# Both parts of the tokens in one 512-column matmul, for z, 13 query blocks and 20 blocks of u

## The chip, the core and the metric

The kernel runs on one core of one Trainium2 chip. The metric is the device time of the core in microseconds: the median of three runs, 2088.07 us before the change (2087.21 to 2090.55). The engines are named as in the profile: PE is the tensor engine's matmuls and PEld its weight loads, ACT the scalar engine, DVE the vector engine, POOL GpSimd, SP the engine that issues most loads.

## The reference

One decoder layer over 256 tokens and 16 meta tokens, width 2048. What the change touches is cut to this:

```python
proj = h @ w_in                       # [pool 1024 | z 3072 | x 3072 | B 1024 | C 1024 | dt 48]
y = y * silu(z)                       # then a gated RMS norm by group, and w_out
h = layer_norm(ALPHA * h + concat(pool_out, ssd_out) @ w_out)
q = h @ wq                            # 8 heads x 2 x 128, product keys, top 16 experts of 16384
act = gelu(h . u_tab[expert])         # here: h @ u.T for all 16384 experts, masked by the gate
out = layer_norm(ALPHA * h + (gate * act) @ v_tab[expert])
```

All of it is fp32.

## The kernel before, in words

PE multiplies fp32 numbers in three passes. Each operand is split into two parts that PE takes at full speed (fp32r): a high part, rounded by ACT, and a low part, the rest, subtracted by DVE. A product is high x high + token low x weight high + token high x weight low.

The weights of w_in, w_out, wq, u and v stream in 512 KB units, in the order of one list, `W_ORDER`. `next_unit()` hands out the next unit's parts `wh` and `wl` (128 x 1024 each) and keeps three units ahead: SP loads `raw`, ACT casts it to `wh` (line 129), DVE subtracts to `wl` (line 130). There are three buffers of each, so a cast waits until PE has passed the `wh` of the unit three earlier.

For the projections, the queries and u the weight tile is PE's stationary operand and the tokens move. The normed tokens stand transposed as 16 chunks of 128 x 272 (`hTH`, `hTL`, from line 196) or 128 x 256 (`h1H`, `h1L`, line 556). `mm_unit` (line 199) takes one unit, half of the contraction (`kh`), in three passes of eight matmuls, all into the left half of one PSUM bank:

```python
for w, xx, first, last in ((wh, xh, ...), (wh, xl, ...), (wl, xh, ...)):
    for k in range(8):
        pe.matmul(ps[:m, :n], w[:, k * m:(k + 1) * m], xx[:, kh * 8 + k, t0:], ...)
```

A block of 128 output rows is two units. The stages, in order:

- w_in: 72 blocks. Eight groups of five x, B and C blocks and three z blocks (line 477, 256 columns each), with the scan's small steps between them as side work (`tick()`). ACT takes silu of z's bank.
- w_out: here the tokens are stationary and 512 columns of `w` move (`wide_pass`, line 497).
- queries: 16 blocks (line 875). The first three are begun while the tokens are still being normed. ACT copies each bank into `qT` (line 885). DVE then finds the top 16 as side work.
- u: 128 blocks (`u_block`, line 612), 64 for each half of the experts. ACT takes gelu of the bank (line 617 or 620); for the second half DVE multiplies the result into the gate's tile `a` (line 622). For the first half the gate comes later. POOL scatters the blocks of `a` to sorted places in memory (line 719), for the second half one block at a time, as they are done; for the first half from line 728, after DVE has numbered the places (line 711).
- v: the sorted rows are loaded by SP (`ac`, line 990), POOL gathers the rows of v that they name (line 995), and PE multiplies with 512 moving columns (line 1032). The parts of a block of `a` are made by ACT and DVE in `v_scr` (lines 1019 and 1020), which takes the place of `h1L`; the residual `rr` takes the place of `h1H` and is loaded by POOL (line 1105). The tiles of the sorted rows take the place of the second half of `a`.

The order of the instructions on each engine comes from a scheduler at build time, except where the code pins it (`keep_in_program_order`).

Of the kernel before, what the change touches and what calls it, by code (L numbers as in the profile page):

```python
# [11 lines left out]
F32 = mybir.dt.float32  # L12
F32R = mybir.dt.float32r
F16 = mybir.dt.float16
U32 = mybir.dt.uint32
AF = mybir.ActivationFunctionType
# [5 lines left out]
P = 128  # L22
NMETA = 16
NL1 = 3
NQ1 = 3
NLB = 4
NDB = 2

HALF = {1: (64, P - NDB, 52, 12, 39), 0: (0, 64, 53, 13, 40)}
TRIPS = 24
# [12 lines left out]
T = 256  # L45
L = NMETA + T
D = 2048
KC = D // P
# [14 lines left out]
def tile_layer(ctx: ExitStack, tc: tile.TileContext, x, meta, pk, pk48, w_in, w_dt, w_pool,  # L63
               w_out, wq, keys, u, v, ln_nat, out):
    nc = tc.nc
    act, dve, pool, pe = nc.scalar, nc.vector, nc.gpsimd, nc.tensor
# [6 lines left out]
    def ps_tile(name):  # L73
        return psp.tile([P, 512], F32, tag="ps", name=name)
# [13 lines left out]
    def slots_of(half):  # L88
        _, _, n, s, e = HALF[half]
        _, _, top, _ = rows_of(half)  # L90
        return ([(half, k, (0, 1)) for k in range(e - s)], [(half, k, (0,)) for k in range(top - s, top)],
                [(half, k, (1,)) for k in range(e - s, n - s)])

    def mixed(*lists):
        at = [((k + 0.5) / len(one), w, one[k]) for w, one in enumerate(lists) for k in range(len(one))]
        return [b for _, _, b in sorted(at, key=lambda z: z[:2])]

    both, a_only, b_only = zip(slots_of(1), slots_of(0))
    V_BLOCKS = [("d", b, (0, 1)) for b in range(P - NDB, P)] + mixed(both[0], a_only[0], b_only[0][:8])
    LOOP_AT = len(V_BLOCKS)  # L100
    V_BLOCKS += mixed(both[1][:-6], a_only[1], b_only[0][8:] + b_only[1][:-NLB])

    LATE = []
    for k, blk in enumerate(both[1][-6:]):
        V_BLOCKS.append(blk)
        if k < NLB:
            LATE.append(len(V_BLOCKS))
            V_BLOCKS.append(b_only[1][k - NLB])
    for i, (what, b, _) in enumerate(V_BLOCKS):
# [6 lines left out]
    def next_unit():  # L116
        while len(issued) < min(used[0] + 1 + AHEAD, len(W_ORDER)):
            src = W_ORDER[len(issued)]
            wp, wb = held.get(len(issued), (wst, 3))
            if isinstance(src, tuple):  # L120
                n = 1024
                raw = gathered(src[0])[:, src[1] * 1024:(src[1] + 1) * 1024]
            else:
                n = src.shape[-1]
                raw = wst.tile([P, 1024], F32, tag="raw", name="raw", bufs=3)
                nc.sync.dma_start(raw[:, :n], src)
            wh = wp.tile([P, 1024], F32R, tag="wh", name="wh", bufs=wb)
            wl = wp.tile([P, 1024], F32R, tag="wl", name="wl", bufs=wb)
            act.copy(wh[:, :n], raw[:, :n])  # L129
            dve.tensor_sub(wl[:, :n], raw[:, :n], wh[:, :n].bitcast(F32))  # L130
            issued.append((wh, wl))
        used[0] += 1
        r = issued[used[0] - 1]
        issued[used[0] - 1] = None
        return r


    side = []

    def tick(n=1):  # L140
        while n and side:
            try:
                next(side[0])
                n -= 1
            except StopIteration:
                side.pop(0)
# [46 lines left out]

    front = ExitStack()
    hTp = front.enter_context(tc.tile_pool(name="hTp", bufs=1))
    hTH = hTp.tile([P, KC, L], F32R, name="hTH")
    hTL = hTp.tile([P, KC, L], F32R, name="hTL")

    def mm_unit(ps, xh, xl, kh, m, n, t0=0):

        wh, wl = next_unit()
        for w, xx, first, last in ((wh, xh, kh == 0, False), (wh, xl, False, False), (wl, xh, False, kh == 1)):
            for k in range(8):
                pe.matmul(ps[:m, :n], w[:, k * m:(k + 1) * m], xx[:, kh * 8 + k, t0:],  # L204
                          start=first and k == 0, stop=last and k == 7)
# [4 lines left out]
    with tc.tile_pool(name="ln0", bufs=1) as lp:  # L210
# [33 lines left out]
        for k in range(KC):  # L244
            ps = ps_tile("pst")
# [5 lines left out]
            if k == KC // 2 - 1:  # L251

                for t0, m in ((0, NH), (14, P), (14, P)):
                    ps = ps_tile("psj")
# [14 lines left out]
    def proj(t0, m=P):  # L269
        if pre:  # L270
            was, ps = pre.pop(0)
            assert was == t0
            tick()
        else:
            ps = ps_tile("psj")
            mm_unit(ps, hTH, hTL, 0, m, L - t0, t0)
            tick()
        mm_unit(ps, hTH, hTL, 1, m, L - t0, t0)
        tick()
        return ps  # L280
# [183 lines left out]
    _, ps = pre.pop(0)  # L464
# [6 lines left out]
    for g in range(NG):  # L471
        bT = conv(24 + g, 0, "bT", 2)
        cc = conv(32 + g, 12, "cc", 2)
        xT = [conv(3 * g + j, 0, "xT", 6) for j in range(3)]
        zs = []
        side.append(group_steps(g, bT, cc, xT, zs))
        for j in range(3):
            pz = proj(NMETA)
            z = sp.tile([P, T], F32, tag="zs", name="zs", bufs=4)
            act.activation(z, pz[:, :T], AF.Silu)  # L480
            zs.append(z)


# [2 lines left out]
    def hold(units, hp):  # L486
        for i in units:
            held[i] = (hp, len(units))
# [60 lines left out]

    lws = ExitStack()  # L550
    h1ps = []

    def w_out_body1(i):
        if i == 0:
            h1ps.append(ctx.enter_context(tc.tile_pool(name="h1p", bufs=1, side="right", reuse_waits="tile")))
            h1ps.append(h1ps[0].tile([P, KC, T], F32R, tag="h1H", name="h1H"))
            h1ps.append(h1ps[0].tile([P, KC, T], F32R, tag="h1L", name="h1L"))
            lw = lws.enter_context(tc.tile_pool(name="lw", bufs=1, side="right", reuse_waits="tile"))
            hold(range(2 + 144 + 64 - NL1, 2 + 144 + 64), lw)

# [10 lines left out]
                dve.bn_stats(sts[tt][:, c], hs[tt][:, cs])  # L571
    lp = lnp[0]
    lws.close()
    h1p, h1H, h1L = h1ps
    mv = lp.tile([P, 2, 2], F32, name="mv1")
    rs = lp.tile([P, 2], F32, name="rs1")
    nb1 = lp.tile([P, 2], F32, name="nb1")
# [12 lines left out]
    for k in range(KC):  # L590
        ps = ps_tile("pst1")
# [20 lines left out]
    def u_block(b):  # L612
        ps = ps_tile("psu")
        for kh in range(2):
            mm_unit(ps, h1H, h1L, kh, P, T)
        if b < 64:
            act.activation(a_half[0][:, b, :T], ps[:, :T], AF.Gelu)
        else:

            act.activation(ps[:, :T], ps[:, :T], AF.Gelu)  # L620
            g = a_half[1][:, b - 64, :T]
            dve.tensor_mul(g if b < P - NDB else a_dense[:, b - (P - NDB)], g, ps[:, :T])  # L622

# [166 lines left out]
    ap1s = ExitStack()  # L790
# [3 lines left out]
    qT = rp.tile([P, 16, T], F32, name="qT")  # L794
# [80 lines left out]
    for j in range(16):  # L875
        if j < NQ1:
            ps = pre[j]
            tick()
        else:
            ps = ps_tile("psq1")  # L880
            mm_unit(ps, h1H, h1L, 0, P, T)
            tick()
        mm_unit(ps, h1H, h1L, 1, P, T)
        tick()
        act.copy(qT[:, j, :], ps[:, :T])
        if j == 0:
            side.append(nat_steps())
            side.append(zero_steps())
        if j % 2:
            side.append(route_steps(j // 2))  # L890
# [3 lines left out]
    ohp = ctx.enter_context(tc.tile_pool(name="ohp", bufs=3))  # L894
    slp = ctx.enter_context(tc.tile_pool(name="slots", bufs=1))
    a_dense = slp.tile([P, NDB, T], F32, name="a_dense")
    ap0s = ExitStack()
# [33 lines left out]
    def rank_0():  # L931
        if flagq:
            flag_tick(2)
        elif ranked[0] is not None:
            next(ranked[0])
            if next(ranked[0]):
                ranked[0] = None

    for b in range(64, 128):
        u_block(b)  # L940
        if pos[1] is not None:
            due = min(b - 64, -(-(P - NDB - 64) * (b - 72) // 50), P - NDB - 64)
            while n_sc[1] < due:
# [11 lines left out]
    while pos[0] is None:  # L955
        rank_0()
    while n_sc[1] < P - NDB - 64:
        scatter(1, n_sc[1])
        n_sc[1] += 1


    rrt = h1p.tile([P, 2, D], F32, tag="h1H", name="rr")
    rr = [rrt[:, tt] for tt in range(2)]
    v_scr = h1p.tile([P, 16, T], F32R, tag="h1L", name="v_scr")
    ap1s.close()
    vp = ctx.enter_context(tc.tile_pool(name="vp", bufs=1, side="right", reuse_waits="tile"))
    st2 = [vp.tile([P, 4, 6], F32, name=f"st2{tt}", bufs=1) for tt in range(2)]
    GA = 3
# [38 lines left out]
    def a_split(i):  # L1007
        what, b, tts = V_BLOCKS[i]

        if i in LATE:  # L1010
            s = 8 + 2 * LATE.index(i)
        else:
            s = 2 * (a_n[0] % (4 if i > LATE[0] - 4 else 8))
            a_n[0] += 1
        ah, al = v_scr[:, s], v_scr[:, s + 1]
        c = slice(tts[0] * P, (tts[-1] + 1) * P)
        src = a_dense[:, b - (P - NDB)] if what == "d" else acs[i]

        tc.keep_in_program_order(act.copy(ah[:, c], src[:, c]))  # L1019
        tc.keep_in_program_order(dve.tensor_sub(al[:, c], src[:, c], ah[:, c].bitcast(F32)))  # L1020
        a_ops[i] = ah, al
# [54 lines left out]
    for i, (what, b, tts) in enumerate(V_BLOCKS):  # L1076
# [13 lines left out]
        if i == 0:  # L1090
            a_split(0)
        if i + 1 < len(V_BLOCKS):
            a_split(i + 1)
# [78 lines left out]
```

## Time and profile before

| what | value |
|---|---|
| median of three runs | 2088.07 us (2087.21 to 2090.55) |
| profiled execution, its own time | 2089.42 us |
| its span, first to last instruction | 2087.7 us |
| mean granted clock of PE | 0.988 |
| z's stage (all eight groups) | about 157 to 520 us |
| queries, after the first three | about 718 to 813 us |
| last 20 blocks of u | about 1469 to 1602.9 us |
| v | from 1603.35 us |

In a timeline row the columns are the start in us, the time in us, engine, line, operation, output<-inputs, partitions and shape, how many, and in brackets the idle time just before with what ended it. A matmul's end is modelled and overlaps the next one's start, so what a matmul costs is read from the distance of two starts and not from its duration.

### The profile page before, as it was taken

How to read it: one execution, taken by the hardware profiler on the slowest of the kernel's cores; microseconds unless marked ns; L12 is line 12 of the kernel's file. 1: busy time of each engine (PE TensorE's matmuls, PEld its weight loads, DVE VectorE, ACT ScalarE, POOL GpSimd, SP SyncE). 2: the span in 40 equal slices, each digit the busy share in tenths (PEclk: the TensorE clock that was granted, in tenths of full speed). 3: DMA queues.
4: the chain of work that ended last, by engine and by line, in shares of the span. 5: the costliest groups of instructions: out<-in, count | busy, mean ns of one | idle time of the engine just before them, and what ended most of it. 6: DMA issues, size and time to landing. Idle time of an engine off the chain costs nothing. (4 is left out here: it accounts for less than half of the span.)

```text
span 2087.7 us, 37525 instructions
## 1 busy us (share of the span) xinstructions
PE 2025.3 (97%) x14780; PEld 1868.7 (90%) x14780; DVE 1571.0 (75%) x2530; ACT 1116.7 (53%) x1637; POOL 525.2 (25%) x423
## 2 busy tenths in 40 slices
PE   7999999999999899999899999999989999999997
PEld 6999999999888899999899999999988778877885
DVE  6777777777754878999899879999834656656667
ACT  6457777777433544445468663333423555555553
POOL 1000000000000000000555426566361672233330
PEclk9999999999999999999999999999989999999999
DMA  4555555555766555556455556666666998778884
GB/s 160 185 180 176 177 177 174 174 177 162 270 228 198 176 185 181 175 177 185 134 156 169 172 180 195 198 185 206 201 192 229 307 324 315 277 258 288 302 298 153
DMA packets 113970, 430.75 MB, mean 206 GB/s; under 512 B 14112, under 2 KB 27808, under 8 KB 98800
## 3 DMA queue, kind: packets, MB, share of 16 engines
q1 hardware_dynamic: 89168, 282.29, 43.8%
q0 software_dynamic: 24336, 145.53, 19.5%
q8 instruction: 116, 1.90, 0.4%
q10 hardware_dynamic: 288, 0.52, 0.1%
q14 instruction: 62, 0.51, 0.1%
HBM read 407.20 MB, written 21.09 MB: 205 GB/s over the span
## 5 line engine op out<-in xcount | busy, mean ns | idle before, releaser
L129 ACT CAST wh<-raw 128x1024 fp32r<-128x1024 f32 (+1 forms) x502 | 525.7, 1047 | 677.4 <-PE psu L204 359.8
L130 DVE TENSOR_TENSOR wl<-raw,wh 128x1024 fp32r<-128x1024 f32 (+1 forms) x502 | 624.4, 1245 | 298.6 <-ACT wh L129 268.1
L130 DVE TENSOR_TENSOR wl<-rawv,wh 128x1024 fp32r<-128x1024 f32 x210 | 256.8, 1224 | 170.6 <-ACT wh L129 155.8
L1032 PE MATMUL psv<-wh,v_scr 128*128 128x512 f32 x1304 | 363.2, 398 | 11.6 <-ACT v_scr L1019 6.6
L129 ACT CAST wh<-rawv 128x1024 fp32r<-128x1024 f32 x210 | 220.3, 1049 | 205.0 <-PE psv L1032 126.9
L761 POOL TENSOR_TENSOR o<-oe,gT 128x512 f16<-128x512 f16 x128 | 204.0, 1604 | 473.6 <-DVE oe L759 291.7
L1032 PEld LDWEIGHTS psv<-wh,v_scr 128*128 128x128 f32 x1304 | 245.8, 189 | 75.5 <-ACT v_scr L1019 8.8
L204 PE MATMUL psu<-h1H,wh 128*128 128x256 f32 x2048 | 296.5, 287 | 2.8 <-issue 2.8
L204 PE MATMUL psu<-h1L,wh 128*128 128x256 f32 x2048 | 290.5, 284 | 3.8 <-issue 3.7
L204 PE MATMUL psu<-h1H,wl 128*128 128x256 f32 x2048 | 288.6, 284 | 0.0
L204 PEld LDWEIGHTS psu<-h1L,wh 128*128 128x128 f32 x2048 | 263.8, 190 | 5.6 <-issue 5.6
L204 PEld LDWEIGHTS psu<-h1H,wh 128*128 128x128 f32 x2048 | 264.6, 191 | 4.0 <-issue 3.9
L204 PEld LDWEIGHTS psu<-h1H,wl 128*128 128x128 f32 x2048 | 264.4, 190 | 0.7 <-issue 0.6
L1032 PE MATMUL psv<-wl,v_scr 128*128 128x512 f32 x652 | 206.6, 396 | 0.0
L995 POOL DMA_INDIRECT rawv<-in_v,ac x105 | 127.3, 1212 | 256.1 <-DVE wl L130 200.0
L719 POOL DMA_INDIRECT acd<-a,flags x126 | 154.5, 1226 | 99.4 <-DVE a L622 58.7
L204 PE MATMUL psj<-hTH,wh 128*128 128x272 f32 (+5 forms) x1168 | 177.3, 294 | 1.3 <-ACT hTH L185 0.8
L204 PE MATMUL psj<-hTH,wl 128*128 128x272 f32 (+5 forms) x1168 | 165.9, 284 | 0.0
L204 PE MATMUL psj<-hTL,wh 128*128 128x272 f32 (+5 forms) x1168 | 165.8, 284 | 0.0
L204 PEld LDWEIGHTS psj<-hTH,wh 128*128 128x128 f32 (+1 forms) x1168 | 154.2, 189 | 5.0 <-ACT hTH L185 1.9
L204 PEld LDWEIGHTS psj<-hTL,wh 128*128 128x128 f32 (+1 forms) x1168 | 151.7, 187 | 0.1
L204 PEld LDWEIGHTS psj<-hTH,wl 128*128 128x128 f32 (+1 forms) x1168 | 151.6, 187 | 0.0
(250 smaller groups left out, 2217.1 us busy)
## 6 DMA issues: line engine op xcount, KB each, us to landing
raw<-in_u SPq DMA_DIRECT2D x256, 512.0 KB
raw<-in_w_in SPq DMA_DIRECT2D x144, 512.0 KB
raw<-in_w_out SPq DMA_DIRECT2D x64, 512.0 KB
raw<-in_wq SPq DMA_DIRECT2D x32, 512.0 KB
ac<-acd SPq DMA_DIRECT2D x105, 128.5 KB
clb<-cd POOLq DMA_DIRECT2D x8, 816.0 KB
x<-in_x SPq DMA_DIRECT2D x4, 512.0 KB
gb<-in_ln_nat POOLq DMA_DIRECT2D x2, 1024.0 KB
```

The lines of the kernel that those rows point to most:

```text
L129: act.copy(wh[:, :n], raw[:, :n])
L130: dve.tensor_sub(wl[:, :n], raw[:, :n], wh[:, :n].bitcast(F32))
L204: pe.matmul(ps[:m, :n], w[:, k * m:(k + 1) * m], xx[:, kh * 8 + k, t0:], start=first and k == 0, stop=last and k == 7)
L719: i = pool.indirect_dma_start(out=acd[half][:, :], out_offset=bass.IndirectOffsetOnAxis(ap=pos[half][:, b:b + 1], axis=0), in_=a_half[half ...
L761: behind[0] = pool.tensor_mul(o1, oe.unsqueeze(2).to_broadcast([P, 4, 2, 64]), gT[:, t0:t0 + 4, :].unsqueeze(3).to_broadcast([P, 4, 2, 64]))
L995: i = pool.indirect_dma_start(out=raw, out_offset=None, in_=v[:, :], in_offset=bass.IndirectOffsetOnAxis(ap=ac.bitcast(U32)[:, T:T + 1], a ...
L1032: pe.matmul(po[tt][n], mm[:, tt * P:(tt + 1) * P], w[:, c:c + 512], start=first, stop=end)
```

## The change

z, the query blocks 3 to 15 and the u blocks 108 to 127 use a new function, `mm_both`. The high and the low tokens are now two halves of one tile (`hT`, `h1`), so that one matmul can move 2 x 256 columns: high tokens to the left half of the bank, low tokens to the right. A unit is then eight matmuls of 512 columns with `wh` and eight of 256 columns with `wl`. In a block's first unit the wide ones come first, in its second unit last. The halves of the bank are added up: ACT copies the right one to SBUF, DVE adds the left one; silu of z, and gelu of u, follow on ACT. Since `h1` is one tile now, `rr` and `v_scr` come from a pool of their own in its place, and the first block of v has its parts in tiles of another pool (`a_first`).

```diff
+U_BOTH = 108
...
+    hT = hTp.tile([P, 2, KC, L], F32R, name="hT")
+    hTH, hTL = hT[:, 0], hT[:, 1]
+
+    def mm_both(ps, xx, kh, t0=0):
...
+        wh, wl = next_unit()
+
+        def low():
+            for k in range(8):
+                pe.matmul(ps[:, :T], wl[:, k * P:(k + 1) * P], xx[:, 0, kh * 8 + k, t0:], start=False, stop=False)
+
+        if kh:
+            low()
+        for k in range(8):
+            pe.matmul(ps, wh[:, k * P:(k + 1) * P], xx[:, :, kh * 8 + k, t0:],
+                      start=kh == 0 and k == 0, stop=kh == 1 and k == 7)
+        if not kh:
+            low()
...
-            pz = proj(NMETA)
+            pz = ps_tile("psz")
+            for kh in range(2):
+                mm_both(pz, hT, kh, NMETA)
+                tick()
             z = sp.tile([P, T], F32, tag="zs", name="zs", bufs=4)
-            act.activation(z, pz[:, :T], AF.Silu)
+            act.copy(z, pz[:, T:])
+            dve.tensor_add(z, z, pz[:, :T])
+            act.activation(z, z, AF.Silu)
...
         for kh in range(2):
-            mm_unit(ps, h1H, h1L, kh, P, T)
+            if b < U_BOTH:
+                mm_unit(ps, h1H, h1L, kh, P, T)
+            else:
+                mm_both(ps, h1, kh)
+        if b >= U_BOTH:
+            part = ohp.tile([P, T], F32, tag="o2", name="part", bufs=2)
+            act.copy(part, ps[:, T:])
+            dve.tensor_add(ps[:, :T], part, ps[:, :T])
...
-        act.copy(qT[:, j, :], ps[:, :T])
...
+            mm_both(ps, h1, 1)
+            tick()
+            act.copy(qT[:, j, :], ps[:, T:])
+            dve.tensor_add(qT[:, j, :], qT[:, j, :], ps[:, :T])
...
-    rrt = h1p.tile([P, 2, D], F32, tag="h1H", name="rr")
+    ap1s.close()
+    h1s.close()
+    vrp = ctx.enter_context(tc.tile_pool(name="vrp", bufs=1, side="right", reuse_waits="tile"))
+    rrt = vrp.tile([P, 2, D], F32, name="rr")
     rr = [rrt[:, tt] for tt in range(2)]
-    v_scr = h1p.tile([P, 16, T], F32R, tag="h1L", name="v_scr")
-    ap1s.close()
+    v_scr = vrp.tile([P, 16, T], F32R, name="v_scr")
...
+        if i == 0:
+
+            ah, al = (ohp.tile([P, T], F32R, tag="o1", name="a_first", bufs=2) for _ in range(2))
```

PE at the end of u and the start of v, before: the last two units of u, then v's first block.

```order
L204 MATMUL psu<-h1H,wh 128x256 x8
L204 MATMUL psu<-h1L,wh 128x256 x8
L204 MATMUL psu<-h1H,wl 128x256 x8
L204 MATMUL psu<-h1H,wh 128x256 x8
L204 MATMUL psu<-h1L,wh 128x256 x8
L204 MATMUL psu<-h1H,wl 128x256 x8
L1032 MATMUL psv<-wh,v_scr 128x512 x10
L1032 MATMUL psv<-wl,v_scr 128x512 x2
```

PE in the same place now (`h_6509` is the tile h1, both parts):

```order
L212 MATMUL psu<-h_6509,wh 128x512 x16
L207 MATMUL psu<-h_6509,wl 128x256 x16
L212 MATMUL psu<-h_6509,wh 128x512 x8
L1074 MATMUL psv<-wh,a_first 128x512 x4
L1074 MATMUL psv<-wl,a_first 128x512 x2
```

Of the sixteen wide ones in the first row eight end the block before. A block's two passes with `wl` stand side by side, and v begins on a tile that is not in the place of h1.

DVE around the last two blocks of u, before (`a_11415` is the second half of a; `a_dense` holds the products of the last two blocks):

```order
L130 TENSOR_TENSOR wl<-raw,wh 128x1024 x2
L622 TENSOR_TENSOR a_dense<-a_11415,psu 128x256
L130 TENSOR_TENSOR wl<-raw,wh 128x1024 x2
L622 TENSOR_TENSOR a_dense<-a_11415,psu 128x256
L1073 TENSOR_LOAD bound
L1020 TENSOR_TENSOR v_scr<-a_dense,v_scr 128x256 x2
```

DVE there now:

```order
L646 TENSOR_TENSOR psu<-part,psu 128x256
L131 TENSOR_TENSOR wl<-raw,wh 128x1024
L653 TENSOR_TENSOR a_dense<-a_10882,psu 128x256
L1115 TENSOR_LOAD bound
L1062 TENSOR_TENSOR a_first<-a_dense,a_first 128x256
L131 TENSOR_TENSOR wl<-raw,wh 128x1024
L646 TENSOR_TENSOR psu<-part,psu 128x256
L653 TENSOR_TENSOR a_dense<-a_10882,psu 128x256
```

The add (line 646) stands between two subtracts of weights; in the last block a subtract stands ahead of the add, and the multiply behind it. ACT's order in the last block is cast, copy, gelu.

POOL's scatters in the last part of u, before (`acd_7642` holds the sorted rows of the second half, `acd_7643` of the first):

```order
L719 DMA acd_7642<-a_11415,flags_12709 8192x257 x9
L719 DMA acd_7643<-a_8718,flags_16501 8192x257 x6
L719 DMA acd_7642<-a_11415,flags_12709 8192x257
L719 DMA acd_7643<-a_8718,flags_16501 8192x257 x8
L719 DMA acd_7642<-a_11415,flags_12709 8192x257
L719 DMA acd_7643<-a_8718,flags_16501 8192x257 x10
L719 DMA acd_7642<-a_11415,flags_12709 8192x257 x8
```

POOL's scatters there now (`acd_7304` is the second half's, `acd_7305` the first's):

```order
L750 DMA acd_7304<-a_10882,flags_12176 8192x257 x9
L750 DMA acd_7305<-a_8185,flags_15968 8192x257 x8
L750 DMA acd_7304<-a_10882,flags_12176 8192x257
L750 DMA acd_7305<-a_8185,flags_15968 8192x257 x10
L750 DMA acd_7304<-a_10882,flags_12176 8192x257
L750 DMA acd_7305<-a_8185,flags_15968 8192x257 x6
L750 DMA acd_7304<-a_10882,flags_12176 8192x257 x8
```

The 24 scatters of the first half are as many as before; two of the second half have moved by two and by four places among them.

## Rows read from the trace of the kernel before

**Rows 1.** The page, part 1: busy us, share of the span, instructions.

```profile
PE 2025.3 (97%) x14780; PEld 1868.7 (90%) x14780; DVE 1571.0 (75%) x2530; ACT 1116.7 (53%) x1637; POOL 525.2 (25%) x423
```

**Rows 2.** Windows: length, busy us and instructions by engine, granted clock, DMA share, GB/s.

```profile
157.00:520.00 363.00, 363.00 (x2969) 348.71 (x2968) 280.03 (x495) 270.40 (x356) 16.23 (x19) 1.00 0.55 174
718.00:813.00 95.00, 95.00 (x802) 95.00 (x801) 69.15 (x176) 41.84 (x56) 0.25 (x1) 1.00 0.63 197
1469.00:1528.00 59.00, 59.00 (x513) 58.88 (x510) 45.23 (x75) 23.84 (x31) 18.79 (x19) 1.00 0.70 209
1528.00:1564.70 36.70, 30.04 (x151) 26.41 (x151) 8.99 (x11) 7.29 (x9) 25.78 (x24) 0.72 0.56 175
```

**Rows 3.** Timeline of PE in z's stage, three passes apart.

```profile
240.62 1.10 PE L204 MATMUL psj<-hTH,wl 128*128 128x256 f32 x8
...
243.44 1.10 PE L204 MATMUL psj<-hTH,wl 128*128 128x256 f32 x8
```

**Rows 4.** Timeline of PE in the query stage, twelve passes apart.

```profile
742.47 1.13 PE L204 MATMUL psq<-h1H,wl 128*128 128x256 f32 x8
...
753.99 1.13 PE L204 MATMUL psq<-h1H,wl 128*128 128x256 f32 x8
```

**Rows 5.** Timeline of PE in u, 36 passes apart; the last is u's last pass.

```profile
1567.57 1.12 PE L204 MATMUL psu<-h1H,wl 128*128 128x256 f32 x8
...
1601.75 1.11 PE L204 MATMUL psu<-h1H,wl 128*128 128x256 f32 x8
```

**Rows 6.** Timeline of PE in the w_out stage, fourteen groups of four apart.

```profile
561.10 1.07 PE L497 MATMUL pso<-wl,mixH 128*128 128x512 f32 x4
...
573.80 1.07 PE L497 MATMUL pso<-wh,mixL 128*128 128x512 f32 x4
```

**Rows 7.** Timeline of PE in the v stage, twelve times six matmuls apart.

```profile
1781.12 1.10 PE L1032 MATMUL psv<-wh,v_scr 128*128 128x512 f32 x4
...
1797.92 1.10 PE L1032 MATMUL psv<-wh,v_scr 128*128 128x512 f32 x4
```

**Rows 8.** Groups by line, ACT of the query stage and u's last 134 us.

```profile
L885 ACT COPY qT<-psq 128x256 f32<-128x256 f32 x15 | 5.5, 370 | 0.0
L622 DVE TENSOR_TENSOR a<-a,psu 128x256 f32<-128x256 f32 x19 | 7.9, 414 | 0.0
L130 DVE TENSOR_TENSOR wl<-raw,wh 128x1024 fp32r<-128x1024 f32 x40 | 49.0, 1225 | 59.9 <-ACT wh L129 32.5 <-issue 15.5 <-remote 11.8
L129 ACT CAST wh<-raw 128x1024 fp32r<-128x1024 f32 x40 | 42.0, 1050 | 83.0 <-PE psu L204 75.7 <-remote 4.0 <-DVE wl L130 1.8
```

**Rows 9.** Timeline of PE, two passes in the slow stretch, four units apart.

```profile
1532.78 0.63 PE L204 MATMUL psu<-h1H,wh 128*128 128x256 f32 x4 [0.17 <-issue]
...
1561.47 2.06 PE L204 MATMUL psu<-h1H,wh 128*128 128x256 f32 x8
```

**Rows 10.** Timeline of POOL, first and last of 28 scatters in a row.

```profile
1521.37 0.97 POOL L719 DMA_INDIRECT acd<-a,flags  x1 [3.02 <-DVE flags L711]
...
1559.44 0.97 POOL L719 DMA_INDIRECT acd<-a,flags  x1 [0.30 <-issue]
```

**Rows 11.** Timelines of ACT, DVE, SP, POOL and PE, end of u.

```profile
1603.20 0.36 ACT L620 ACTIVATE psu<-psu 128x256 f32<-128x256 f32 x1
...
1604.17 0.41 DVE L622 TENSOR_TENSOR a_dense<-a,psu 128x256 f32<-128x256 f32 x1
...
1604.66 19.79 SPq L990 DMA_DIRECT2D ac<-acd  x9
...
1603.16 1.15 POOL L1105 DMA_DIRECT2D rr<-h1d  x2 [8.72 <-PE psu L204]
...
1612.49 1.00 POOL L995 DMA_INDIRECT rawv<-in_v,ac  x1 [8.19 <-DMA ac<-acd]
...
1619.51 0.79 PE L1032 MATMUL psv<-wh,v_scr 128*128 128x512 f32 x1 [4.75 <-ACT v_scr L1019]
```

**Rows 12.** DMA queues from 1602.9 to 1612: packets, MB, share of 16 engines.

```profile
q0 software_dynamic: 288, 2.10, 61.5%
```

More of the change, by code (lines that the diff above doesn't have):

```diff
@@ L195, in tile_layer @@
     hTp = front.enter_context(tc.tile_pool(name="hTp", bufs=1))
-    hTH = hTp.tile([P, KC, L], F32R, name="hTH")
-    hTL = hTp.tile([P, KC, L], F32R, name="hTL")
+    hT = hTp.tile([P, 2, KC, L], F32R, name="hT")
[12 more added lines that the diff above has]
+            low()
     def mm_unit(ps, xh, xl, kh, m, n, t0=0):
@@ L551, in tile_layer @@
     h1ps = []
+    h1s = ExitStack()
     def w_out_body1(i):
         if i == 0:
-            h1ps.append(ctx.enter_context(tc.tile_pool(name="h1p", bufs=1, side="right", reuse_waits="tile")))
-            h1ps.append(h1ps[0].tile([P, KC, T], F32R, tag="h1H", name="h1H"))
-            h1ps.append(h1ps[0].tile([P, KC, T], F32R, tag="h1L", name="h1L"))
+            h1ps.append(h1s.enter_context(tc.tile_pool(name="h1p", bufs=1, side="right", reuse_waits="tile")))
+            h1ps.append(h1ps[0].tile([P, 2, KC, T], F32R, name="h1"))
             lw = lws.enter_context(tc.tile_pool(name="lw", bufs=1, side="right", reuse_waits="tile"))
@@ L573, in tile_layer @@
     lws.close()
-    h1p, h1H, h1L = h1ps
+    _, h1 = h1ps
+    h1H, h1L = h1[:, 0], h1[:, 1]
     mv = lp.tile([P, 2, 2], F32, name="mv1")
@@ L880, in tile_layer @@
             ps = ps_tile("psq1")
-            mm_unit(ps, h1H, h1L, 0, P, T)
+            mm_both(ps, h1, 0)
             tick()
-        mm_unit(ps, h1H, h1L, 1, P, T)
-        tick()
-        act.copy(qT[:, j, :], ps[:, :T])
+        if j < NQ1:
+            mm_unit(ps, h1H, h1L, 1, P, T)
+            tick()
+            act.copy(qT[:, j, :], ps[:, :T])
+        else:
+            mm_both(ps, h1, 1)
+            tick()
+            act.copy(qT[:, j, :], ps[:, T:])
+            dve.tensor_add(qT[:, j, :], qT[:, j, :], ps[:, :T])
         if j == 0:
```

## The prediction

> **What bounds the kernel now.** I read the busy shares first, then the stages where the change works, then the tensor engine's own rows there. The page gives PE 97% of the span [rows 1]. Over z's stage and over the query stage the windows [rows 2] show PE busy in every microsecond (363.00 of 363.00, 95.00 of 95.00) with DVE at 77% and 73%, and in u's blocks 108 to 117 (1469 to 1528 us) PE at 100% and DVE at 77%. So there a saving on PE is a saving of time, if what is added to ACT and DVE stays beside it. One stretch differs: from 1528 to 1564.7 PE is busy 30.04 of 36.70 us at a granted clock of 0.72. It lies inside the last 20 blocks of u, which the change edits.
>
> **What a matmul costs, by its width.** In z three passes of eight 256-column matmuls start 2.82 us apart [rows 3]: 0.940 us a pass, 117.5 ns each. In the query stage twelve passes take 11.52 us [rows 4]: 120.0 ns each. In u 36 passes take 34.18 us [rows 5]: 118.7 ns. The clock is full in all three. For 512 columns there are two prices: 56 matmuls of the w_out stage in 12.70 us [rows 6], 226.8 ns, and 72 of the v stage in 16.80 us [rows 7], 233.3 ns. At 2.4 GHz 256 columns alone are 106.7 ns and 512 are 213.3, so each matmul carries 11 to 20 ns that are not columns. The change keeps the columns of a unit (24 x 256 = 8 x 512 + 8 x 256) and takes out eight matmuls, hence eight of these extras.
>
> **Part 1, the matmuls.** I take 226.8 ns for the wide one: like u's it uses the tensor engine without a gap and without new operands in between; the v stage's price is the upper neighbour.
> - z: 24 blocks are 48 units. Before 24 x 117.5 = 2820 ns, now 8 x 226.8 + 8 x 117.5 = 2754: 66 ns, 3.2 us in all.
> - queries: 13 blocks, 26 units. 2880 to 8 x 226.8 + 960 = 2774: 106 ns, 2.8 us.
> - u: 20 blocks, 40 units, of which 4 to 5 run in the slow stretch and are taken as unchanged. For 35: 2849 to 8 x 226.8 + 950 = 2764: 85 ns, 3.0 us.
>
> Sum 9.0 us. Bounds: if the wide matmul has only z's own extra (213.3 + 10.8 = 224.1 ns) z gives 87, queries 128, u 106 ns a unit: 4.2 + 3.3 + 3.7 = 11.2 us. At the v stage's 233.3 they give 14, 54 and 33 ns: 0.7 + 1.4 + 1.2 = 3.3 us. If it cost as much as two of z's narrow ones, 235 ns, z would give nothing, queries 1.0 and u 0.7 us: 1.7 us.
>
> The Trainium skill, "TensorE: Matmul & The Clock Gate", section "Back-to-back issue gap", gives a gap of columns at 2.4 GHz plus about 2.5 ns; eight matmuls fewer would then be 20 ns a unit and the sum 2.3 us over 114 units instead of 9.0. The trace disagrees with that size in every stage above (extras of 11 ns and more).
>
> **Part 2, adding the halves.** Each new ACT copy of 256 columns is 0.37 us and each DVE add 0.41 us [rows 8]. z: 24 adds are 9.9 us on DVE, which has 83 us free; 24 copies 8.9 us on ACT, which has 93. Queries: 13 adds, 5.4 us on a DVE with 26 free; the ACT copy there only reads the other half. u: 20 copies and adds, 7.4 and 8.3 us, on engines with 13.8 (DVE) and 35 us (ACT) free in the first ten blocks alone. I cost them at nothing; what hides them is PE's full stage. If DVE filled up, its 57 adds would cost up to 23.6 us.
>
> **Part 3, the waits.** The add waits on ACT's copy, which waits for the block's last matmul, and the casts and subtracts of the next weights are queued behind them. A unit of the second half of k now wants wl first, at its start. Its cast can begin after the wide pass of the unit three earlier (8 x 226.8 = 1.8 us in); cast 1.05, subtract 1.23, an add before it 0.41: done at 4.5 us, wanted at 3 x 2.76 = 8.3. So 3.8 us are spare; before, with the cast after two passes (1.9) and wl wanted in the third pass, it was done at 4.2 and wanted at 10.4, 6.2 spare. DVE's other work has to be over 3.8 us late before PE waits. The cast for a unit of the first half now waits for the end of the unit three earlier (2.76), its wh is there at 3.8 and its wl at 5.05, wanted at 8.3 and 10.1. Nothing.
>
> Table loads on ACT fall from 81 to 74 in the program; ACT does not bound, so nothing.
>
> **Part 4, the end of u.** PE's last pass starts at 1601.75 and its result is there at 1602.86 (call it E). Then gelu at 1603.20 on ACT, the multiply at 1604.17 on DVE, and only then SP issues the first load of the sorted rows at 1604.66, E + 1.8, because those tiles take the place of a half of a. The gather waits for that load until 1612.49, and PE stands 4.75 us before 1619.51 [rows 11]. Now ACT's order is cast, copy, gelu and DVE's is subtract, add, multiply: 0.1 + 1.05 + 1.23 + 0.41 + 0.36 + 0.41, and the hops, is E + 3.7. So SP issues 1.9 us later. But POOL's two loads of rr start right after E and fill the queues: 2.10 MB of q0 by 1612, 61.5% of all engines' time [rows 12]; the sorted rows can hardly move before they are through. Cost between 0 and 1.9 us; nearer to 0 because of that row: 0.5. What a_first saves in front of v's first block only lengthens PE's later wait: nothing.
>
> **Sum.** 9.0 - 0.5 = 8.5 us. Against the profiled execution (2089.42 us, span 2087.7) that is 2080.9. That execution is 1.35 us above the median of the runs, so 2079.6 against 2088.07.
>
> **The slow stretch.** POOL issues 28 scatters back to back from 1521.37 to 1559.44 [rows 10]; from 1532.78 to 1561.47 PE runs four units in 28.69 us, 7.17 each instead of 2.85 [rows 9], with pauses inside passes that the profile puts down to issue, and a lower clock [rows 2]. It costs 4 x 4.3 = 17 us. I do not know by what PE is slowed there, so both directions are rivals.
>
> **The rivals.**
> 1. *The extra goes with the columns, not with the matmul*, so that taking out eight matmuls saves next to nothing (a wide one at 233 to 235 ns). For: the v stage's rows. Against: w_out's rows, steady over 56 matmuls. Saving 1.7 to 3.3 us, less 0.5: 2086.9 to 2085.3. Chance 0.14. The rule of the Trainium skill quoted in part 1 comes out here as well, 2.3 - 0.5 us, 2086.3, and the trace bears it out only as far as these rows do.
> 2. *The stretch gets shorter.* If what is slow goes by instruction, 16 matmuls instead of 24 take 7.17 x 16/24 = 4.8 us a unit: 4 x 2.4 = 9.6 us more, 2070. For: the pauses come between matmuls, not at the start of a pass. Against: at half clock the columns alone are 5.1 us of the 7.17. Chance 0.14.
> 3. *The stretch gets longer: slower.* In it DVE's add waits for the end of a block whose matmuls crawl, the next subtract stands behind the add, and every second unit now begins with that wl: a loop through PE, ACT and DVE in place of one with 3.8 us to spare. Each further unit at 7.17 instead of 2.76 us costs 4.4 us; with two the gain is gone (2088.4), from three on it decides: 2092.8. For: PE has nothing to spare there, and the change adds two hops to the loop. Against: POOL's burst has as many scatters as before, and it is the burst that starts and ends the stretch. Chance 0.12.
>
> The forecast has 0.57; 0.03 is left for what I do not see. About 0.2% (4.2 us) is what a measurement of this kernel can tell from no change: faster is below 2083.9. That holds the forecast nearly whole, rival 2 and a little of the rest: 0.72. Rival 1 is the middle: 0.15. Rival 3 and half of the rest: 0.13. The range reaches down to rival 2 (2070) and up through rival 1 (2087); rival 3 stays out. The forecast alone reaches from 2076.9 (11.2 us, nothing lost at the end of u) to 2083.9 (230 ns, half way to the v stage's price: 6.1 us, less the whole 1.9).
>
> **What would show it.** Passes of eight wide matmuls starting 1.81 us apart in z, queries and u (1.87 would be rival 1). PE still busy all of 157 to 518 us. Start of v some 9 us earlier than 1603.35, PE's stop before the third v block 5 to 7 us instead of 4.75. Four to five units at about 7 us in the burst; two fewer or three more would make the prediction wrong, as would PE waits on wl anywhere in z or the queries.

## The result and the profile after

The changed kernel takes 2077.73 us (median of six runs, 2073.08 to 2081.63) against 2089.59 us for the kernel before in the same set (2087.21 to 2093.11): a ratio of 0.9941, 95% interval 0.9925 to 0.9958, so some 12 us faster. The forecast was 2079.6 us. The total came out near it, but by other terms than the forecast had, so by luck. The profiled execution took 2078.22 us, its span is 2076.5 us.

The page's busy shares, as [rows 1]:

```profile
PE 2016.6 (97%) x13868; PEld 1818.7 (88%) x13868; DVE 1586.2 (76%) x2587; ACT 1120.2 (54%) x1674; POOL 531.6 (26%) x423
```

912 matmuls fewer are 114 units times eight. The windows of [rows 2], after:

```profile
157.00:520.00 363.00, 363.00 (x2639) 332.49 (x2638) 284.69 (x518) 270.35 (x372) 16.79 (x20) 1.00 0.53 173
718.00:813.00 95.00, 95.00 (x603) 85.77 (x602) 74.64 (x194) 42.37 (x56) 0.26 (x1) 1.00 0.61 195
1469.00:1528.00 59.00, 58.99 (x353) 51.06 (x352) 47.46 (x84) 27.44 (x41) 19.67 (x18) 1.00 0.67 206
1528.00:1564.70 36.70, 32.51 (x157) 26.32 (x157) 12.61 (x17) 10.76 (x18) 27.07 (x25) 0.91 0.70 220
```

PE is still full in the first three: the adds and copies are hidden. The fourth holds the difference: PE at a granted clock of 0.91 in place of 0.72. The timelines of PE in z, in the queries and near the end of u, as [rows 3 to 5]:

```profile
172.96 2.02 PE L212 MATMUL psz<-hT,wh 128*128 128x512 f32 x8
174.82 1.11 PE L207 MATMUL psz<-hT,wl 128*128 128x256 f32 x8
...
734.17 3.88 PE L212 MATMUL psq<-h,wh 128*128 128x512 f32 x16
737.90 0.51 PE L207 MATMUL psq<-h,wl 128*128 128x256 f32 x3
...
1578.17 3.88 PE L212 MATMUL psu<-h,wh 128*128 128x512 f32 x16
1581.88 2.06 PE L207 MATMUL psu<-h,wl 128*128 128x256 f32 x16
```

A pass of eight wide matmuls takes 1.86 us from start to start, 232.5 ns each; over all their distances in the trace the mean is 232.0 ns in z (336), 232.7 in the queries (192), 232.7 in u (275). That is the v stage's price [rows 7], not the 226.8 ns of w_out [rows 6].

Where the span's 11.2 us went, from the starts of PE's first or last matmul of each stage in the two traces:

| stretch | before, us | after, us | won, us |
|---|---|---|---|
| to the first matmul of w_out (holds z) | 509.82 | 509.13 | 0.7 |
| w_out, to the first transpose | 181.02 | 181.63 | -0.6 |
| transposes and queries, to u's first matmul | 104.93 | 102.85 | 2.1 |
| u, to the last ranking matmul (psl) | 719.49 | 719.93 | -0.4 |
| from there to v's first matmul, "the tail" | 88.09 | 77.74 | 10.4 |
| v and the end | 484.37 | 485.21 | -0.8 |

So nearly all of it came from the tail of u, where the slow stretch lies. PE in that stretch after, as [rows 9]:

```profile
1543.61 2.59 PE L207 MATMUL psu<-h,wl 128*128 128x256 f32 x16
1546.31 2.17 PE L212 MATMUL psu<-h,wh 128*128 128x512 f32 x8
1548.87 1.42 PE L212 MATMUL psu<-h,wh 128*128 128x512 f32 x5 [0.39 <-issue]
...
1558.48 5.73 PE L212 MATMUL psu<-h,wh 128*128 128x512 f32 x16
1564.04 1.11 PE L207 MATMUL psu<-h,wl 128*128 128x256 f32 x8
1565.85 0.39 PE L207 MATMUL psu<-h,wl 128*128 128x256 f32 x1 [0.70 <-DVE wl L131]
```

The pauses by "issue" and the low clock are there again. From 1543.61 to 1564.04 two blocks, four units, are slow: 20.4 us instead of 2 x 5.62, 5.1 us a unit. Before, four units were slow as well, at 7.17 us each [rows 9]. They come late in POOL's row of scatters, which is about as long as before (41.7 us, 38.1 in [rows 10]):

```profile
1519.50 0.97 POOL L750 DMA_INDIRECT acd<-a,flags  x1 [6.67 <-DVE cs L738]
...
1561.16 1.23 POOL L750 DMA_INDIRECT acd<-a,flags  x1 [0.30 <-issue]
```

Before, PE paused from 1532.3 us on, 11 us after the row began; now from 1544.4, 25 us after it began. The granted clock fell to its lower level (1.2 GHz) only after the pauses had begun: before, from 1537.0 us on and for 20.5 us in all; now from 1555.4 us on and for 6.8 us.

The end of u, as [rows 11]:

```profile
1591.28 1.09 PE L1074 MATMUL psv<-wh,a_first 128*128 128x512 f32 x4
1591.48 1.05 ACT L130 CAST wh<-raw 128x1024 fp32r<-128x1024 f32 x1 [0.63 <-PE psu L212]
1591.75 1.15 POOL L1147 DMA_DIRECT2D rr<-h1d  x2 [4.53 <-PE psu L212]
...
1592.43 0.37 ACT L645 COPY part<-psu 128x256 f32<-128x256 f32 x1
...
1594.56 0.42 DVE L653 TENSOR_TENSOR a_dense<-a,psu 128x256 f32<-128x256 f32 x1 [0.43 <-ACT psu L651]
...
1595.06 3.21 SPq L1029 DMA_DIRECT2D ac<-acd  x7
...
1600.55 1.00 POOL L1034 DMA_INDIRECT rawv<-in_v,ac  x1 [7.65 <-DMA ac<-acd]
...
1607.70 0.79 PE L1074 MATMUL psv<-wh,v_scr 128*128 128x512 f32 x1 [5.15 <-ACT v_scr L1061]
```

ACT goes on at 1591.48 with PE's last result, and SP issues 3.6 us later (1.8 before).

### The profile page after: what moved, and what is told of

Read it like the earlier page. It is cut to its first block, busy times and chain, and to the rows that moved or that the text cites. A ratio compares the mean times of both kernels' runs of the same rounds, so it can differ in the third digit from the quotient of the medians.

```text
span 2076.5 us, 35859 instructions
## 1 busy us (share of the span) xinstructions
PE 2016.6 (97%) x13868; PEld 1818.7 (88%) x13868; DVE 1586.2 (76%) x2587; ACT 1120.2 (54%) x1674; POOL 531.6 (26%) x423
## 5 line engine op out<-in xcount | busy, mean ns | idle before, releaser
L222 PE MATMUL psu<-h,wh 128*128 128x256 f32 x3456 | 454.5, 284 | 0.0
L222 PEld LDWEIGHTS psu<-h,wh 128*128 128x128 f32 x3456 | 426.4, 189 | 0.1
L222 PE MATMUL psu<-h,wl 128*128 128x256 f32 x1728 | 240.0, 281 | 0.0
L222 PE MATMUL psj<-hT,wh 128*128 128x272 f32 (+4 forms) x1568 | 219.8, 292 | 1.3 <-ACT hT L186 0.8
L222 PEld LDWEIGHTS psu<-h,wl 128*128 128x128 f32 x1728 | 220.3, 188 | 0.0
L222 PEld LDWEIGHTS psj<-hT,wh 128*128 128x128 f32 (+1 forms) x1568 | 203.3, 188 | 4.8 <-ACT hT L186 2.0
L788 DVE TENSOR_TENSOR o<-iota,iT 128x512 f16<-128x512 f16 x128 | 149.9, 1198 | 1.5 <-PE pg L803 1.5
L1074 PEld LDWEIGHTS psv<-wl,v_scr 128*128 128x128 f32 x644 | 122.1, 190 | 28.9
L222 PE MATMUL psj<-hT,wl 128*128 128x272 f32 (+4 forms) x784 | 112.9, 286 | 0.0
L222 PEld LDWEIGHTS psj<-hT,wl 128*128 128x128 f32 (+1 forms) x784 | 103.0, 186 | 0.1
```

Source lines behind the costliest of these rows:

```text
L788: dve.tensor_tensor(o2, iota[:, None, :].to_broadcast([P, 4, P]), i2.to_broadcast([P, 4, P]), ALU.is_equal)
L1074: pe.matmul(po[tt][n], mm[:, tt * P:(tt + 1) * P], w[:, c:c + 512], start=first, stop=end)
```

## The experiments

The question was what shortened the tail, and whether the wide matmul's price holds. Every set of runs has its own runs of the kernel before. The stretch turned out to come and go: in the first set the kernel before took 2094.79 us, in the four later ones 2071.60, 2072.53, 2071.26 and 2071.17, the 2072.53 on the chip of the first set. The kernel before was not profiled again in the later sets, but no profile of another kernel there shows pauses inside u's passes. The expectations on record call this "two kinds of chip"; that one chip gave both does not bear that out. Below, "the first period" is the first set, and "the calm period" the later ones.

**z and the queries alone** (first period).

```diff
-U_BOTH = 108
+U_BOTH = 128
```

> z and the 13 query blocks as changed, all 128 blocks of u as before. Readings of the traces so far: z won some 0.5 us and the queries some 2.1 us, and about 10 us came from u's last 20 blocks, above all from the slow stretch during POOL's scatters. All theories below: 2086 to 2088 us, 2 to 3 us under the kernel before, slow stretch with four units at 7.17 us as before (POOL's order of scatters is the old one here). Rival of them all (the stretch's length hangs on when it begins, not on u's code): the stretch is shorter here too, 2078 to 2081.

Measured: 2090.54 us against 2094.79, 0.9978 (0.9962 to 0.9993), 4.6 us less. Its profile has the long stretch. The window 1520 to 1570 us (columns as in [rows 2]) shows it:

```profile
1520.00:1570.00 50.00, 38.42 (x227) 34.70 (x226) 12.89 (x15) 10.89 (x14) 29.15 (x28) 0.76 0.56 176
```

The expected 2 to 3 us lie inside the interval; the 2086 to 2088 us themselves were missed, with a slower kernel before in this set. u begins here at 792.69 us, a little earlier than in the changed kernel (793.61), and the stretch is no shorter, which speaks against the rival that its length hangs on when it begins.

**u alone** (first period): z and the queries call `mm_unit` again, u stays as changed. One place of the edit:

```diff
-            mm_both(ps, h1, 0)
+            mm_unit(ps, h1H, h1L, 0, P, T)
...
```

> z and the queries as before, u's blocks 108 to 127 as changed. If the gain sits in u: 2079 to 2081 us, the slow stretch some 8 us shorter than before. If it hangs on when the stretch begins (which the earlier stages shift by 2 us): no more than 2 us under the kernel before.

Measured: 2083.07 us, 0.9936 (0.9908 to 0.9963), 13.4 us less, but between 2069.37 and 2090.74 in seven runs. So u's edit carries most of the gain in that period. The profiled run is the slowest of the seven, and in it the stretch is long:

```profile
1520.00:1570.00 50.00, 39.70 (x189) 31.55 (x188) 18.97 (x34) 15.47 (x24) 31.12 (x29) 0.83 0.62 189
```

PE's first and last rows of the slow part there:

```profile
1544.29 2.39 PE L212 MATMUL psu<-h,wh 128*128 128x512 f32 x9
...
1571.15 2.06 PE L207 MATMUL psu<-h,wl 128*128 128x256 f32 x16
```

Between these starts lie 48 matmuls, three units: 9.0 us a unit, more than before the change.

**Two narrow matmuls for a wide one** (first period): order of the passes, adds and tiles as changed, 24 matmuls in a unit as before.

```diff
-        for k in range(8):
-            pe.matmul(ps, wh[:, k * P:(k + 1) * P], xx[:, :, kh * 8 + k, t0:],
-                      start=kh == 0 and k == 0, stop=kh == 1 and k == 7)
+        for q in range(2):
+            for k in range(8):
+                pe.matmul(ps[:, q * T:(q + 1) * T], wh[:, k * P:(k + 1) * P], xx[:, q, kh * 8 + k, t0:],
+                          start=kh == 0 and q == 0 and k == 0, stop=kh == 1 and q == 1 and k == 7)
```

> As the changed kernel, but each 512-column matmul is made as two of 256 columns with the same weight tile (high tokens for all eight chunks, then low), so that 24 matmuls make a unit as before; the order of the passes, the adds and POOL's new order of scatters stay. Theory 1 (the slow stretch goes by PE's instructions): the stretch is as long as before, the z and query gains are gone, 2089 to 2091. Theory 2 (the stretch shrank by POOL's new order of scatters, or by the new order of the passes and their buffers): the stretch is as short as in the changed kernel, 2080 to 2082.

Measured: 2092.85 us, 0.9987 (0.9962 to 1.0012): level with the kernel before, though its runs lie between 2078.01 and 2109.52. Level is what theory 1 said, though not at its 2089 to 2091 us. The profiled run is one of the slower ones; PE there:

```profile
1541.13 0.64 PE L213 MATMUL psu<-h,wh 128*128 128x256 f32 x4 [0.86 <-issue]
1542.56 0.75 PE L213 MATMUL psu<-h,wh 128*128 128x256 f32 x5 [0.79 <-issue]
1544.00 0.52 PE L213 MATMUL psu<-h,wh 128*128 128x256 f32 x3 [0.68 <-issue]
1545.44 0.28 PE L213 MATMUL psu<-h,wh 128*128 128x256 f32 x1 [0.92 <-issue]
...
1561.10 0.58 PE L207 MATMUL psu<-h,wl 128*128 128x256 f32 x1 [0.85 <-issue]
```

A few matmuls, then a pause, then a few more, through two passes. The new order of POOL's scatters and of the passes is in this kernel too, and it does not win the time. The two kernels of this set that have the wide matmul in u do: their intervals (0.9908 to 0.9963 for u alone, 0.9916 to 0.9964 for the next one) hardly touch this one.

**Both parts of a chunk side by side** (first period), so that the wide matmul reads one piece of 512 columns. `hT` and the indices in `mm_both` are changed in the same way.

```diff
-            h1ps.append(h1ps[0].tile([P, 2, KC, T], F32R, name="h1"))
+            h1ps.append(h1ps[0].tile([P, KC, 2, T], F32R, name="h1"))
```

> As the changed kernel, but the high and the low part of a chunk of tokens lie side by side, so that a wide matmul moves 512 columns in one piece rather than two pieces of 256. If the pieces cost the 6 ns by which a wide matmul (232.5 ns) lies above w_out's (226.8 ns): passes of eight 1.81 us apart in place of 1.86, 114 units x 8 x 5.7 ns = 5.2 us less, 2072 to 2073. If the price is that of 512 columns with a new weight tile for each matmul: passes 1.86 us apart, 2077 to 2078.

Measured: 2080.52 us, 0.9940 (0.9916 to 0.9964), as the changed kernel. The matmul's price is the same, 3.73 us for sixteen, 233.1 ns:

```profile
736.18 3.88 PE L212 MATMUL psq<-h,wh 128*128 128x512 f32 x16
739.91 1.11 PE L207 MATMUL psq<-h,wl 128*128 128x256 f32 x8
```

The two pieces cost nothing. Why w_out's 512-column matmuls take 226.8 ns and all others 232 to 234 stays open.

**No first-half scatters in u, four per block in v** (calm period), in both kernels.

```diff
-                for _ in range(3):
+                for _ in range(0):
...
-        for _ in range(2 if i > 1 else 0):
+        for _ in range(4 if i > 1 else 0):
```

> The kernel before, but the 24 scatters of the first half that stood in u's last blocks are issued in v instead (four per block of v in place of two), so that POOL's row of 28 scatters is broken up; 19 scatters of the second half stay in u. If POOL's row of scatters is what slows PE: the stretch (about 17 us) is gone or nearly, 2073 to 2079 us, and the runs lie closer together. If PE is slowed in v just as much by the moved scatters: about as before. If the row of scatters is not the cause: the pauses stay where they were, as before.

> The changed kernel with the same edit. If the row of scatters slows PE, what is left of the change is what the matmuls give (z 0.7, queries 2.1, u some 1.8 us): 4 to 5 us under the edited kernel before, 2069 to 2075. If the change's 10 us in u have another cause than the stretch: 11 to 13 us under the edited kernel before.

Measured: 2107.42 and 2102.08 us against 2071.60, 1.0164 (1.0143 to 1.0185) and 1.0140 (1.0118 to 1.0163). Both missed. There was no stretch to remove in this period, and v paid: PE's waits in the kernel before so edited (us in total, times, longest), and in the changed one:

```profile
PE psv L1032 <- ACT v_scr L1019: 29.1, 15, 4.9
```

```profile
PE psv L1074 <- ACT v_scr L1061: 28.5, 13, 5.7
```

With two scatters per block these waits are 7.8 us in the changed kernel and 6.6 in the kernel before. v, from PE's restart after the stop to its last matmul, went from 457 to 495 and 492 us. The waits make some 22 of these 38 and 34 us. The clock fell as well: in the kernel before so edited PE had a granted clock of 0.87 over 91 us of v, where the kernel before had 1.00 (1667 to 1758 us):

```profile
1650.00:1741.00 91.00, 70.03 (x241) 50.93 (x241) 34.65 (x40) 30.33 (x42) 66.23 (x60) 0.87 0.72 248
```

Between the two edited kernels lie 5.3 us, near the 4 to 5 expected of the matmuls.

**The wide matmul only beside the row of scatters** (calm period): blocks 116 to 122 of u, z and the queries as before.

```diff
-U_BOTH = 108
+U_BOTH = (116, 123)
...
-            if b < U_BOTH:
+            if not U_BOTH[0] <= b < U_BOTH[1]:
```

> z and the queries as before; of u only blocks 116 to 122, those beside POOL's row of scatters, use the wide matmul. If the gain is the shorter stretch: 7 to 9 us under the kernel before, nearly all that u's 20 blocks gave. If u's gain lies in all 20 blocks alike: 7/20 of it, 3 to 5 us.

Measured: 2072.63 us against 2071.60, 1.0002 (0.9987 to 1.0017). Neither number: with no stretch to shorten, seven blocks at 0.08 us each are 0.6 us, which is not to be seen.

**The changed kernel again** (calm period).

> The changed kernel as it is, beside the others on this chip: 11 to 13 us under the kernel before, with a spread of 5 us or more between its runs, since the stretch does not always have the same length.

Measured: 2066.10 us (2062.57 to 2071.94) against 2071.60, 0.9975 (0.9963 to 0.9987), 5.2 us less instead of 12. The same window, changed kernel in its first profile and in this one:

```profile
1520.00:1570.00 50.00, 45.11 (x228) 37.19 (x227) 21.70 (x29) 18.55 (x29) 35.90 (x32) 0.93 0.69 219
```

```profile
1520.00:1570.00 50.00, 50.00 (x285) 43.59 (x284) 27.49 (x36) 23.25 (x36) 39.12 (x33) 1.00 0.88 265
```

PE is full at the full clock, although POOL's row of scatters runs in this profile too, 34 of them:

```profile
1517.63 0.97 POOL L750 DMA_INDIRECT acd<-a,flags  x1 [6.66 <-DVE cs L738]
...
1567.90 0.97 POOL L750 DMA_INDIRECT acd<-a,flags  x1 [0.30 <-issue]
```

So the row by itself does not slow PE.

**No first-half scatters in u, v at two per block for longer** (calm period).

```diff
-                for _ in range(3):
+                for _ in range(0):
```

> The kernel before with no first-half scatter in u; v issues two per block as before, for 12 blocks more (instead of four per block). So POOL has one scatter per 5.7 us in u's last blocks. Two kinds of chip have been met: one where the kernel before takes some 2090 to 2095 us with PE's slow stretch in the profile, and one where it takes 2071.6 us and the profiles show none. If POOL's row of scatters brings the stretch about on the first kind: there 15 to 20 us under the kernel before, 2071 to 2076, with runs that lie closer together; on the second kind no difference (within 3 us). If the stretch has another cause: no difference on either. If the 24 scatters cost as much in v: slower on both by 10 us and more.

> The changed kernel with the same edit. If the row of scatters is the cause, what the change gives beside it is what the matmuls give on every chip: 4 to 6 us under the edited kernel before, 2066 to 2071; against the kernel before that is 20 to 25 us on the first kind of chip and about 5 on the second.

> The kernel before without first-half scatters in u, once more, in the hope of a chip on which the kernel before has the slow stretch (2088 us and more). There: if POOL's row of scatters brings the stretch about, 2071 to 2076, 15 to 20 us under the kernel before, and a profile without pauses in u; if it has another cause, as the kernel before, with the pauses where they were. On a chip where the kernel before takes 2071 to 2073 us: no difference, as already seen.

Measured: 2073.66 us against 2072.53 for the kernel before so edited, 1.0008 (0.9994 to 1.0022), and again 2073.30 against 2071.26, 1.0016 (1.0004 to 1.0027); 2067.14 for the changed kernel so edited, 0.9976 (0.9962 to 0.9991). With two per block v takes all 64 scatters at next to no cost, 1 to 2 us by the medians. Both tries fell into the calm period, so whether the row is needed for the stretch was not tested.

**Two narrow for a wide one again** (calm period).

> Two 256-column matmuls in place of each wide one, once more. Where the kernel before takes 2071 to 2073 us (no slow stretch), the changed kernel is 5 us under it. If those 5 us are the price of the wide matmul (232 to 233 ns against two of 117.6 to 118.7): this kernel is level with the one before, 2071 to 2074. If a part of them comes from the rest of the change (order of the passes, new tiles for the start of v): 2067 to 2070. Where the kernel before takes 2088 us and more: level with it again, by a stretch as long as before, with runs 10 us and more apart.

Measured: 2074.08 us against 2071.17, 1.0012 (1.0002 to 1.0022), level with the kernel before or 2.5 us over it. So the gain of the calm period is the wide matmul's. Between this ratio and the changed kernel's 0.9975 lie 7.7 us, 3 to 12 by the ends of the two intervals; the price worked out in the next section gives 3.7. Here a block's 32 matmuls with `wh` take 3.80 us where sixteen wide ones take 3.71:

```profile
1576.32 3.96 PE L213 MATMUL psu<-h,wh 128*128 128x256 f32 x32
1580.12 2.06 PE L207 MATMUL psu<-h,wl 128*128 128x256 f32 x16
```

**The tails side by side.** From the last ranking matmul to v's first, with PE's first pause and POOL's row, in the profiles of the first period (and the two of the result):

| kernel | tail, us | row of scatters, us | first pause after the row's start, us |
|---|---|---|---|
| before | 88.1 | 1521.4 to 1559.4 | 10.9 |
| z and queries alone | 91.9 | 1519.0 to 1554.1 | 8.9 |
| two narrow for a wide | 91.6 | 1524.2 to 1561.5 | 15.8 |
| changed | 77.7 | 1519.5 to 1561.2 | 24.9 |
| u alone | 85.1 | 1523.9 to 1562.6 | 22.3 |
| side by side | 86.4 | 1521.9 to 1558.4 | 21.1 |

In the calm period the tail is 68.5 and 69.1 us with narrow matmuls and 67.6 with wide ones. In all six the pauses begin inside POOL's row and stop within 7 us of its last scatter. With wide matmuls they begin later, and in all six the granted clock falls 4 to 11 us after the first pause. The pauses have a beat of their own: in five of the six (in the changed kernel less strictly) the starts that end a pause by "issue" are mostly one, two or three times 0.71 to 0.72 us apart (1541.13 to 1545.44 in the rows of the two narrow matmuls above), while POOL's scatters there start 1.28 us apart. So a pause is not the work of one scatter. What sets this beat is not shown.

## Why the prediction was right in its sum and wrong in its terms

**Part 1, the matmuls: mis-sized.** The step that failed is "I take 226.8 ns for the wide one: like u's it uses the tensor engine without a gap and without new operands in between". It measured 232.0 to 232.7 ns, close to rival 1's 233 to 235, in all three stages, and about the same with the columns in one piece. With it a unit wins 8 x (2 x 117.6 - 232.0) = 26 ns in z and 8 x (2 x 118.7 - 232.7) = 38 ns in the queries and u: 1.2 + 1.0 + 1.5 = 3.7 us instead of 9.0. (The 120.0 ns of [rows 4] are a short stretch; over all narrow matmuls of the queries the mean is 118.6 to 119.3 ns, by the profile.) In the table of stretches z won 0.7 us and the queries 2.1; why these differ from 1.2 and 1.0 is not shown. The calm period's ratio, 5.2 us with an interval of 2.7 to 7.7, holds that sum. By these two widths most of what a matmul takes beyond its columns grows with the columns; what goes with each matmul is 3 to 5 ns (2 x 117.6 - 232.0 and 2 x 118.7 - 232.7), not 11 to 20. The Trainium skill's rule ("TensorE: Matmul & The Clock Gate", section "Back-to-back issue gap": about 2.5 ns on top of the columns, for an isolated matmul) gives 215.8 ns for 512 columns, far under these rows. As a price for one matmul taken out it came closer: the 2.3 us in part 1 of the prediction are nearer to 3.7 than its 9.0.

**Part 2, the adds: right.** PE is busy all of 157 to 520 and of 718 to 813 us, DVE there at 78 and 79%.

**Part 3, the waits: right.** There is no PE wait on `wl` in z or the queries, and one of 0.70 us in u, behind the slow stretch.

**Part 4, the end of u: near, nothing for 0.5.** SP issues 1.8 us later than before after PE's last result, as worked out (1.9), but PE's restart after the stop comes no later: 16.7 us after the start of u's last matmul (1591.04), 16.9 before (1602.57). That the full queues hide the later issue fits, but no run shows it by itself. v begins 0.5 us sooner after u than before, and from its first matmul to the restart it is 16.4 us instead of 16.2: what `a_first` saves does lengthen the wait. The stop is 5.15 us, inside the 5 to 7 expected.

**The slow stretch: wrong.** Of u's 40 units the prediction had "4 to 5 run in the slow stretch and are taken as unchanged", and it gave the shortening (rival 2) 0.14. In the pair of profiles four units were slow, as forecast, but at 5.1 us each instead of 7.17, near the 4.8 of rival 2. By the tails, against those of the calm period (69.1 is that of the kernel before without first-half scatters in u), the stretch's cost shrank from 88.1 - 69.1 = 19.0 us to 77.7 - 67.6 = 10.2 us, by 8.8 us, near the 9.6 of rival 2. So rivals 1 and 2 happened together, and 3.7 + 8.8 = 12.5 us is near the result's 11.9 (11.2 between the profiles). v's start, 12.07 us earlier than 1603.35 instead of some 9, is the sign of it. The forecast had 8.5 us: 5 too many in the matmuls and nothing in the stretch, where 9 were won. That these two errors partly cancel is luck. Rival 3, a longer stretch, did not happen.

What the runs show of rival 2's reason ("if what is slow goes by instruction"): with the wide matmul the kernels won 12 to 13 us by their ratios where the stretch was there (u alone, side by side, the result), 8 us and more beyond their matmuls; with the same code but two narrow ones, nothing. That is what the reason asks for. It is not shown why. A slow unit has no fixed price by its instructions: with 16 matmuls it took 5.1 us in the result's profile, but 9.0 in u alone and 9.4 with the parts side by side (1542.32 to 1570.47 us, three units). With wide matmuls the stretch also began later. The times of one kernel lay more than 10 us apart, and the profiled runs of three of these kernels are among their slowest, so that times and not tails carry the verdict. What PE is paused by, and why it was gone in the later sets, for the kernel before too by its time, stays open. A row of 33 or 34 scatters alone does not do it.

## What to carry to other kernels

Before costing an edit that joins two matmuls into one, split the price of a matmul into a part by columns and a part by matmul from two widths in the same stage with the same kind of operands; a price from another stage can hide which it is. Where a stage of the profile runs slow for an unknown reason, measure the kernel before in several sets of runs first: here the kernel before itself differed by some 20 us between sets, more than the change, and more than half of the gain of one set was not there in the others. Small work that must go somewhere (here the scatters) can cost next to nothing at two per block and 36 us at four: try the lower rate over a longer time first.

## What was not expected

- PE's pauses in u are a condition that comes and goes: the kernel before took 2089.59 and 2094.79 us in two sets and 2071.17 to 2072.53 in four others, with the same row of scatters in its program.
- A 512-column matmul costs 232 to 234 ns in four stages and 226.8 in w_out, at the same granted clock; one piece or two of moving columns makes no difference.
- Moving 24 scatters into v costs 1 to 2 us by the medians at two per block of v, and 36 us at four, some 22 of them in PE's waits for the parts of `a`, with a lower granted clock beside them.
